# Retention with one transposition, the sample's tile at 128 rows, and scale sums in banks of their own

## The chip, the cores and the metric

The kernel runs on one core of a Trainium2 chip. The metric is device time in microseconds, from one execution's start to its end; the median of three runs stands for a kernel, and one more execution is taken by the hardware profiler. The engines are named as in the profile: PE multiplies matrices (PEld is its loading of the stationary operand), DVE and ACT work element by element and can read PE's results in PSUM, POOL works element by element in SBUF only, and SP issues most DMAs. PSUM has eight banks of 512 fp32 columns on 128 partitions.

## The reference

One layer of a streaming encoder, for 1024 frames of a new stream (the prompt) and 32 frames of a running one (the sample, behind 512 cached frames). Both go through the same weights. Cut to what matters:

```python
z = rmsnorm(x, g_norm) @ w_in                 # q, k, v of attention; q, k, v, gate of retention; 2 branch gates
o_a = diff_attn(qa, ka, va)                   # per head two softmax maps: p1 - lam * p2, times v; 8 heads
o_r = retention(qr, kr, vr)                   # per head, rotary q and k of 64, v of 128
x = x + (sigmoid(gate_a) * o_a + sigmoid(gate_r) * o_r) @ w_o
h = rmsnorm(x, g_ffn)
x = x + (silu(h @ w_ff_gate) * (h @ w_ff_up)) @ w_ff_down
x = x + sigmoid(rmsnorm(x, g_ple) @ w_ple_gate) * (p @ w_ple)

def retention_chunk(q, k, v, s0, d_mat, q_decay):
    inner = einsum('ihd,jhd->hij', q, k) * d_mat
    o = einsum('hij,jhe->ihe', inner, v)
    return o + einsum('ihd,hde->ihe', q, s0) * q_decay
```

For the prompt the state `s0` goes from chunk to chunk; for the sample it is an input. The outputs are y of both streams, the new keys and values, and the new retention states.

## The kernel before

Everything is computed to fp32's accuracy: the large products split each operand into two fp16 parts and add three fp16 matmuls (`mm3`, L471 to L473; in the first stage L713 to L715), after scaling weights by a power of two that is found from their size at run time. Transpositions and retention use fp32 on PE.

**First stage** (about the first 1,070 us): 8 heads times 9 tiles of tokens. Tiles 0 to 7 are 128 prompt tokens each; tile 8 (`i == NT - 1`) is the 32 sample tokens (`TS = 32`). For each tile there are two units. `unit_a` takes the projection's first half (attention's q, k, v, retention's q, k), norms it, splits and transposes q and k (L1045), and calls `attend`: scores (L850, L853), maximum (DVE, L860), its scaling (L862), exponential (ACT, L868, into tiles named `p`), the difference of the two maps (DVE, in place in the first map's tile), its transposition (L897) and evacuation into two fp16 parts `aT` (L904 or L906, L908), and the product with the values (L916, L917, L920). `unit_b`, four tiles behind, takes the second half (retention's v, the gates), calls `retention`, and merges both branches; the merged tile `mx` is transposed (L1208), split (L1212, L1214) and written to DRAM by SP. The number of rows of a tile is `R`, 128 or, for the sample, 32; matmuls of the sample's tile thus use 32 rows of the contraction or 32 columns of the stationary operand. For the sample `project` multiplies with weights as the stationary operand (L724), and `fold` adds the parts (L735, L737) and transposes four blocks of 32 columns back (L740).

`retention` finds a tile's rotated keys, queries and a block of zeros in `qk[..., 0:192]` as [k | q | 0]. Two transpositions (L1116), of columns 0 to 127 and 64 to 191, give [kT; qT] and [qT; 0]; one copy of both (`copy`, L388, on DVE or ACT) takes them to SBUF as `qT`. Then follow the product of k and q (L1126), the state's share (L1128), the state's increment (L1129), the mask (DVE, L1132) and the product with v (L1134). The zeros let a contraction over 128 partitions act on the 64 of q alone.

**Second stage** (from about 1,080 us): the output projection in four chunks of tokens (352, 352, 176, 176), each followed by `residual` (DVE L1524 adds to x; the sum of squares on ACT and DVE; the norm's sum over partitions on PE, L1543 and L1558; the scaling by it, DVE L1562, which reads that sum in PSUM), then the gate and up projections of 22 blocks in a scheme with 7 products for 8 (`gu_pair`, with combinations of weights on POOL, L1581, of activations, L1472, and of results, L1705 to L1720), then the first two output blocks of the down projection. `load_gu` loads and splits a block's weights: squares on ACT (L1601), their two sums added (DVE L1605), the sum over partitions on PE (`weight_scale`, L300), the power of two (L230, L234), and the split (ACT, DVE L1576). There are seven banks for products (pool `psb`, token "ps") and one, `ssb`, for the norms' sums; L300 puts its sum into column 511 of `ssb`. What an instruction waits for beyond its data follows from the tiles: accesses of one bank by different engines are kept in order.

**Third stage**: the rest of the down projection, and the last gate.

**What sets the order.** In the first two stages each piece of work is a generator that yields what it needs: an engine with an estimated time (`M`, `V`, `S`, `G` for PE, DVE, ACT, POOL), a token of a buffer ("get", "put"), an event or a delay. `Flow.run` picks the earliest by these estimates, and the instructions are issued in that order; each engine works through its own in order and waits where the data isn't there. So a changed estimate, a new token or a new instruction changes the written order of everything behind it in its stage. In `Flow`, the scale sums of the second stage hold a token "sw" of their own, and `residual` one named "ss"; that both use one bank isn't in the estimates.

Of the kernel before, what the change touches and what calls it, by code (L numbers as in the profile page):

```python
# [11 lines left out]
F32 = mybir.dt.float32  # L12
# [58 lines left out]
def M(us):  # L71
    return {"M": us}
# [111 lines left out]
def kernel(  # L184
# [104 lines left out]
    def weight_scale(amax, n, gi, tag, pool=True, norm=False, total=False, at_bank=None):  # L289
# [3 lines left out]
        if total:  # L293
            if at_bank is None:
                yield ("wait", "id")
            key, psum = at_bank or ("o", ps_o)
            yield ("get", key)
            yield M(0.06)
            ps = psum[:, 511:512] if at_bank else psum.tile([P, 512], F32, tag=key, name="mt")[:, 0:1]
            nc.tensor.matmul(out=ps, lhsT=ones16, rhs=amax, start=True, stop=True)  # L300
# [184 lines left out]
    with ExitStack() as pa:  # L485
# [35 lines left out]
        qk = hp.tile([P, NQ, 192], F32, name="qk")  # L521
        nc.gpsimd.memset(qk[:, :, P:], 0.0)
        S2 = hp.tile([P, 2, P], F32, name="S2")
        nc.gpsimd.memset(S2[64:128], 0.0)
        s02 = hp.tile([P, 2, P], F32, name="s02")
        nc.gpsimd.memset(s02[64:128], 0.0)
# [200 lines left out]
        def fold(i, ps):  # L727

            if i < NT - 1:
                return ps, "pj"  # L730
            yield ("get", "su")
            yield S(P)
            su = wk.tile([P, 2, 4, TS], F32, tag="su", name="su", bufs=1)
            psv = ps[:, 0:8 * TS].rearrange("p (g a c) -> p g a c", g=4, a=2)
            nc.scalar.copy(su[:, 1], psv[:, :, 1])  # L735
            yield V(P)
            nc.vector.tensor_tensor(out=su[:, 0], in0=psv[:, :, 0], in1=su[:, 1], op=ALU.add)  # L737
            yield M(0.5)
            for g in range(4):
                nc.tensor.transpose(out=ps[0:TS, g * P:g * P + P], in_=su[:, 0, g], identity=id32)  # L740
            yield ("put", "su")
            return ps, "pj"
# [96 lines left out]
        def attend(key, i, R, q4, sblocks, masked, vblocks, NK, sc_ap, do_ap):  # L839
# [3 lines left out]
            for ms in ((0, 1),) if NK <= 512 else ((0,), (1,)):  # L843
# [19 lines left out]
                for m in ms:  # L863
                    yield ("get", "p")
                    yield S(NK, 0.14)
                    pt = pp_.tile([P, 1024], F32, tag="p", name="p")
                    p0 = 512 * ms.index(m)
# [22 lines left out]
            for j0 in range(0, nb_, 4):  # L890
# [4 lines left out]
                for j in js:  # L895
                    n = vblocks[j][0]
                    nc.tensor.transpose(out=pt[0:n, j - j0, 0:R], in_=p0[:, j * P:j * P + n], identity=id32[0:R, 0:R])  # L897
# [86 lines left out]
        def unit_a(h, i, ps, dA, e):  # L984
            R = P if i < NT - 1 else TS
# [36 lines left out]
            nc.sync.dma_start(out=kvo[h, t0:t0 + R], in_=kv[0:R])  # L1022
# [27 lines left out]
            copy(g, kT[:, :, t0:t0 + R], ptv[:, 2:6, 0:R])  # L1050
# [58 lines left out]
        def retention(h, i, R, vr, e, box):  # L1109
            yield ("wait", ("rot", h, i))  # L1110
            yield ("get", "o")
            yield M(0.22)
            pr = ps_o.tile([P, 512], F32, tag="o", name="pr")

            for a in range(2):
                nc.tensor.transpose(out=pr[:, a * P:a * P + R], in_=qk[0:R, (h * NT + i) % NQ, 64 * a:64 * a + P], identity=id32[0:R, 0:R])  # L1116
# [9 lines left out]
            nc.tensor.matmul(out=pr[0:R, 256:256 + R], lhsT=qT[:, 0, 0:R], rhs=qT[:, 1, 0:R], start=True, stop=True)  # L1126
# [10 lines left out]
            gT = _f((1.0 - 2.0 ** (-5 - h)) ** R)  # L1137
# [15 lines left out]
        def unit_b(h, i, ps, dB, e):  # L1153
            R = P if i < NT - 1 else TS
# [52 lines left out]
            pt = ps_o.tile([P, 512], F32, tag="o", name="t")[:, 0:R]  # L1207
            nc.tensor.transpose(out=pt, in_=mx[0:R], identity=id32[0:R, 0:R])  # L1208
# [3 lines left out]
            nc.scalar.activation(mt[:, 0, 0:R], pt, AF.Copy, scale=smx)  # L1212
            yield V(P, 1.0, 0.06)
            nc.vector.scalar_tensor_tensor(out=mt[:, 1, 0:R], in0=pt, scalar=smx, in1=mt[:, 0, 0:R],  # L1214
                                           op0=ALU.mult, op1=ALU.subtract)
            nc.sync.dma_start(out=mix_d[h, :, :, t0:t0 + R], in_=mt[:, :, 0:R])
# [216 lines left out]
    with ExitStack() as pc:  # L1433
# [18 lines left out]
        with ExitStack() as pw:  # L1452
# [9 lines left out]
            ssb = pss.tile([P, 512], F32, tag="ss", name="ss")  # L1462
# [48 lines left out]
            def residual(c):  # L1511
# [29 lines left out]
                ps = ssb  # L1541
# [42 lines left out]
            def load_gu(j):  # L1584
# [22 lines left out]
                s, d = yield from weight_scale(am, 1, 1, "gu", norm=True, total=True, at_bank=("sw", ssb))  # L1607
# [24 lines left out]
            def load_dn(m):  # L1632
# [25 lines left out]
                s, d = yield from weight_scale(am, 1, None, "dn", norm=True, total=True, at_bank=("sw", ssb))  # L1658
# [161 lines left out]
            flow = Flow(dict(ps=7, ss=1, sw=1, w=3, st=2, pr=2, th=2, acc=2, sq=2))  # L1820
# [210 lines left out]
```

## Time and profile before

| what | value |
|---|---|
| median of 3 runs | 1944.28 us (1943.98 to 1944.51) |
| profiled execution | 1944.48 us |
| its span, first to last instruction | 1942.7 us |
| PE, DVE, ACT, POOL busy | 1886.0, 1511.3, 1065.4, 688.8 us |
| PE's matmuls and loads | 14267 each |
| granted TensorE clock | 0.995 |

A busy time is the time in which an engine had at least one instruction in work. Matmuls overlap, so the duration of one is longer than its share of PE. A form such as "128*32 128x512" of a matmul is rows of the contraction by columns of the stationary operand, and then the moving operand.

### The profile page before, as it was taken

The numbers are of one execution on the slowest core, as the hardware profiler recorded it, in microseconds if no ns is written. First come the engines' busy times: TensorE is split into PE (matmuls) and PEld (weight loads), VectorE is DVE, ScalarE is ACT, GpSimd is POOL, SyncE is SP. The second block draws the span as 40 slices with busy tenths as digits, with TensorE's granted clock in tenths as the row PEclk, the third lists the DMA queues.
The fourth block names the chain that finished last, engine by engine and source line by source line (L and its number), as shares of the span: only waits on it lengthen the run. The fifth ranks groups of instructions, "written<-read, shape, count | busy, mean of one in ns | idle before, by whom it ended". The sixth has DMA issues, their size and how long they took to land.

```text
span 1942.7 us, 38400 instructions
## 1 busy us (share of the span) xinstructions
PE 1886.0 (97%) x14267; PEld 1219.2 (63%) x14267; DVE 1511.3 (78%) x3947; ACT 1065.4 (55%) x2788; POOL 688.8 (35%) x1169
## 2 busy tenths in 40 slices
PE   6899999999999999999999998999999999999999
PEld 3465555655555555556566685777777776666665
DVE  7888878787787777877887579999999986753364
ACT  6766666666666666665666345555555552111132
POOL 2654435454444454444542058322323210000010
PEclk9999999999999999999999998999999999999999
DMA  6222112111121121221113721222111107211031
GB/s 205 70 64 75 62 28 63 57 49 63 33 79 57 31 82 36 55 80 29 61 57 132 267 68 34 78 89 86 69 66 45 66 31 266 73 61 64 24 131 49
DMA packets 71947, 147.43 MB, mean 76 GB/s; under 512 B 25264, under 2 KB 52016, under 8 KB 63824
## 3 DMA queue, kind: packets, MB, share of 16 engines
q1 hardware_dynamic: 71760, 144.98, 22.4%
q8 instruction: 112, 1.84, 0.4%
q14 instruction: 75, 0.61, 0.1%
HBM read 113.61 MB, written 31.34 MB: 75 GB/s over the span
## 4 chain that ended last, share of the span: by engine, by line
PE 77%; DVE 11%; POOL 5%; ACT 4%; issue 2%; DMA 1%; SPq 0%; POOLq 0%; DVEq 0%; ACTq 0%
PE ps L471 9%; PE ps L472 9%; PE ps L473 9%; PE pj L713 8%; PE pj L715 8%; PE pj L714 8%; PE ps L1448 4%; PE ps L1447 4%; PE ps L1446 4%; ACT p L868 2%; PE sc L850 1%; PE t L897 1%; PE sc L853 1%; POOL qkr L749 1%; DVE nm L860 1%
## 5 line engine op out<-in xcount | busy, mean ns | idle before, releaser
L713 PE MATMUL pj<-w,xh 128*128 128x512 f16 x1024 | 390.1, 381 | 0.0
L714 PE MATMUL pj<-w,xh 128*128 128x512 f16 x1024 | 389.5, 380 | 0.0
L715 PE MATMUL pj<-w,xh 128*128 128x512 f16 x1024 | 389.3, 380 | 0.0
L471 PE MATMUL ps<-mixs,w 128*128 128x352 f16 (+1 forms) x960 | 261.9, 278 | 1.2 <-ACT pws L1324 1.2
L472 PE MATMUL ps<-mixs,w 128*128 128x352 f16 (+1 forms) x960 | 261.9, 278 | 0.0
L473 PE MATMUL ps<-mixs,w 128*128 128x352 f16 (+1 forms) x960 | 261.8, 278 | 0.0
L471 PEld LDWEIGHTS <-w 128*128 128x128 f16 x1728 | 170.2, 98 | 63.9 <-ACT mixs L1478 6.4
L473 PEld LDWEIGHTS <-w 128*128 128x128 f16 x1728 | 170.0, 98 | 54.2 <-issue 2.7
L472 PEld LDWEIGHTS <-w 128*128 128x128 f16 x1728 | 169.9, 98 | 51.7 <-issue 2.2
L715 PEld LDWEIGHTS <-xh 128*128 128x128 f16 x1024 | 100.4, 98 | 121.9 <-issue 1.7
L1581 POOL TENSOR_TENSOR st<-st 128x512 f32<-128x512 f32 x66 | 85.8, 1301 | 251.1 <-DVE w L1576 187.0
L868 ACT ACTIVATE p<-sc,nb,scs 128x256 f32<-128x256 f32 (+7 forms) x128 | 106.1, 829 | 83.3 <-POOL nb L862 61.1
L713 PEld LDWEIGHTS <-xh 128*128 128x128 f16 x1024 | 101.2, 99 | 76.3 <-issue 2.8
L472 PE MATMUL ps<-tT,w 128*128 128x352 f16 (+1 forms) x528 | 143.7, 277 | 2.6 <-DVE tT L1472 2.6
L714 PEld LDWEIGHTS <-xh 128*128 128x128 f16 x1024 | 100.4, 98 | 71.7 <-issue 1.1
L471 PE MATMUL ps<-tT,w 128*128 128x352 f16 (+1 forms) x528 | 143.8, 277 | 0.0
L473 PE MATMUL ps<-tT,w 128*128 128x352 f16 (+1 forms) x528 | 143.6, 277 | 0.0
L1576 DVE SCALAR_TENSOR_TENSOR w<-st,gus,w 128x512 f16<-128x512 f32 x132 | 140.5, 1065 | 0.1
L860 DVE TENSOR_REDUCE nm<-sc 128x2 f32<-128x256 f32 (+6 forms) x112 | 102.7, 917 | 24.1 <-PE sc L853 22.0
L1448 PE MATMUL ps<-a,w 128*128 128x352 f16 x312 | 97.5, 313 | 0.5 <-DVE w L1667 0.5
L1446 PE MATMUL ps<-a,w 128*128 128x352 f16 x312 | 97.5, 312 | 0.0
L1447 PE MATMUL ps<-a,w 128*128 128x352 f16 x312 | 97.5, 312 | 0.0
(430 smaller groups left out, 4856.1 us busy)
## 6 DMA issues: line engine op xcount, KB each, us to landing
st<-in_win_dram SPq DMA_DIRECT2D x30, 1024.0 KB, 5.0
st<-in_wgu_dram SPq DMA_DIRECT2D x22, 1024.0 KB, 4.9
st<-in_wdn_dram SPq DMA_DIRECT2D x16, 704.0 KB, 4.6
out_dram<-kv SPq DMA_DIRECT2D x64, 128.0 KB, 1.7
a_d<-a SPq DMA_DIRECT2D x9, 528.0 KB, 2.7
b<-a_d SPq DMA_DIRECT2D x9, 528.0 KB, 8.9
mixs<-mix_d SPq DMA_DIRECT2D x8, 528.0 KB, 5.8
pw_d<-pws SPq DMA_DIRECT2D x12, 352.0 KB, 5.0
```

The source lines that it names most:

```text
L471: nc.tensor.matmul(out=ps, lhsT=wh, rhs=ah, start=first, stop=False)
L472: nc.tensor.matmul(out=ps, lhsT=wh, rhs=al, start=False, stop=False)
L473: nc.tensor.matmul(out=ps, lhsT=wl, rhs=ah, start=False, stop=last)
L713: nc.tensor.matmul(out=ps, lhsT=xhi, rhs=w[:, k, 0], start=(k == 0), stop=False)
L714: nc.tensor.matmul(out=ps, lhsT=xhi, rhs=w[:, k, 1], start=False, stop=False)
L715: nc.tensor.matmul(out=ps, lhsT=xh[:, k, 1, t0:t0 + P], rhs=w[:, k, 0], start=False, stop=(k == KD - 1))
L860: nc.vector.tensor_reduce(out=nm[0:R, mc], in_=pv, axis=AX.X, op=ALU.max, negate=True)
L868: nc.scalar.activation(pt[0:R, 0:NK], ps[0:R, p0:p0 + NK], AF.Exp, bias=nb[0:R, m:m + 1], scale=sc_ap[0:R], accum_out=Z[0:R, m:m + 1])
L1446: nc.tensor.matmul(out=ps, lhsT=wt[:, 0, j], rhs=a[:, 0, cs], start=(first and j == js[0]), stop=False)
L1447: nc.tensor.matmul(out=ps, lhsT=wt[:, 1, j], rhs=a[:, 0, cs], start=False, stop=False)
L1448: nc.tensor.matmul(out=ps, lhsT=wt[:, 2, j], rhs=a[:, 1, cs], start=False, stop=(last and j == js[-1]))
L1576: nc.vector.scalar_tensor_tensor(out=w[:, i, 1], in0=src, scalar=s, in1=w[:, i, 0], op0=ALU.mult, op1=ALU.subtract)
```

## The change

In `retention` the zeros leave `qk`, which is now [k | q]. One transposition gives [kT; qT]. Two copies take it out: the q half, partitions 64 to 127, goes to partitions 0 to 63 of one of two standing tiles `qz`, whose lower 64 partitions were set to zero at the start, and the whole goes to `qT`. The products use `qz` where they used the second transposition.

The sample's tile is handled as 128 rows: `R` is 128 everywhere in `unit_a`, `unit_b`, `attend` and `retention`, and a new `RT`, 32 for the sample, is used where results are written to memory or to a shared tile. `fold` transposes from a standing tile `suz` of four blocks of 128 columns, of which columns 32 to 127 stay zero, so the tile's rows 32 to 127 are zero from there on. The last block of keys and values of the sample has 128 rows in place of 32, and 96 columns of the first map's tile `p` are set to zero by POOL for it.

In the second stage `weight_scale` takes a fresh bank for each sum: one of the seven of the products for the first four blocks of the gate and up projections, and the norms' own for the later ones and for the down projection. The token "sw" goes; the sums now hold "ps" or "ss". `residual` takes its bank per chunk.

```diff
@@ weight_scale
-            ps = psum[:, 511:512] if at_bank else psum.tile([P, 512], F32, tag=key, name="mt")[:, 0:1]
+            ps = psum.tile([P, 512], F32, tag=key, name="mt")[:, 0:1]
@@ tiles of the first stage
-        qk = hp.tile([P, NQ, 192], F32, name="qk")
-        nc.gpsimd.memset(qk[:, :, P:], 0.0)
+        qk = hp.tile([P, NQ, P], F32, name="qk")
+        qz = [hp.tile([P, P], F32, name="qz%d" % j) for j in range(2)]
+        for j in range(2):
+            nc.gpsimd.memset(qz[j][64:128], 0.0)
...
+        suz = hp.tile([P, 4, P], F32, name="suz")
+        nc.gpsimd.memset(suz, 0.0)
@@ fold
-            su = wk.tile([P, 2, 4, TS], F32, tag="su", name="su", bufs=1)
+            su = wk.tile([P, 4, TS], F32, tag="su", name="su", bufs=1)
             psv = ps[:, 0:8 * TS].rearrange("p (g a c) -> p g a c", g=4, a=2)
-            nc.scalar.copy(su[:, 1], psv[:, :, 1])
+            nc.scalar.copy(su, psv[:, :, 1])
             yield V(P)
-            nc.vector.tensor_tensor(out=su[:, 0], in0=psv[:, :, 0], in1=su[:, 1], op=ALU.add)
+            nc.vector.tensor_tensor(out=suz[:, :, 0:TS], in0=psv[:, :, 0], in1=su, op=ALU.add)
             yield M(0.5)
             for g in range(4):
-                nc.tensor.transpose(out=ps[0:TS, g * P:g * P + P], in_=su[:, 0, g], identity=id32)
+                nc.tensor.transpose(out=ps[:, g * P:g * P + P], in_=suz[:, g], identity=id32)
@@ attend
                     pt = pp_.tile([P, 1024], F32, tag="p", name="p")
+                    if NK % P and not m:
+                        nc.gpsimd.memset(pt[:, NK:NK + P - NK % P], 0.0)
...
-                    nc.tensor.transpose(out=pt[0:n, j - j0, 0:R], in_=p0[:, j * P:j * P + n], identity=id32[0:R, 0:R])
+                    nc.tensor.transpose(out=pt[0:n, j - j0, 0:R], in_=pm[0][0:R, j * P:j * P + n], identity=id32[0:R, 0:R])
@@ unit_a (unit_b likewise, with RT in its write of mixT)
-            R = P if i < NT - 1 else TS
+            R, RT = P, P if i < NT - 1 else TS
...
-            nc.sync.dma_start(out=kvo[h, t0:t0 + R], in_=kv[0:R])
+            nc.sync.dma_start(out=kvo[h, t0:t0 + RT], in_=kv[0:RT])
...
-            copy(g, kT[:, :, t0:t0 + R], ptv[:, 2:6, 0:R])
+            copy(g, kT[:, :, t0:t0 + RT], ptv[:, 2:6, 0:RT])
...
-                vblocks.append((TS, vh[0:TS, i, 0], vh[0:TS, i, 1]))
+                vblocks.append((P, vh[:, i, 0], vh[:, i, 1]))
@@ retention
-            yield M(0.22)
+            yield M(0.11)
             pr = ps_o.tile([P, 512], F32, tag="o", name="pr")
-            for a in range(2):
-                nc.tensor.transpose(out=pr[:, a * P:a * P + R], in_=qk[0:R, (h * NT + i) % NQ, 64 * a:64 * a + P], identity=id32[0:R, 0:R])
-            qT = wk.tile([P, 2, P], F32, tag="qT", name="qT")
-            g = yield either(V(256), S(256, -0.06))
-            copy(g, qT[:, :, 0:R], pr[:, 0:2 * P].rearrange("p (a c) -> p a c", a=2)[:, :, 0:R])
+            nc.tensor.transpose(out=pr[:, 0:P], in_=qk[:, (h * NT + i) % NQ], identity=id32)
+            q0 = qz[(h * NT + i) % 2]
+            g = yield either(V(128), S(128, -0.06))
+            copy(g, q0[0:64], pr[64:128, 0:P])
+            g = yield either(V(128), S(128, -0.06))
+            qT = wk.tile([P, P], F32, tag="qT", name="qT")
+            copy(g, qT, pr[:, 0:P])
...
-            nc.tensor.matmul(out=pr[0:R, 256:256 + R], lhsT=qT[:, 0, 0:R], rhs=qT[:, 1, 0:R], start=True, stop=True)
+            nc.tensor.matmul(out=pr[:, 256:384], lhsT=qT, rhs=q0, start=True, stop=True)
             if S_in is not None:
-                nc.tensor.matmul(out=por, lhsT=qT[:, 1, 0:R], rhs=S_in, start=True, stop=False)
-            nc.tensor.matmul(out=pr[:, 384:512], lhsT=qk[0:R, (h * NT + i) % NQ, 0:P], rhs=vr[0:R], start=True, stop=True)
+                nc.tensor.matmul(out=por, lhsT=q0, rhs=S_in, start=True, stop=False)
+            nc.tensor.matmul(out=pr[:, 384:512], lhsT=qk[:, (h * NT + i) % NQ], rhs=vr, start=True, stop=True)
@@ unit_b
-            pt = ps_o.tile([P, 512], F32, tag="o", name="t")[:, 0:R]
-            nc.tensor.transpose(out=pt, in_=mx[0:R], identity=id32[0:R, 0:R])
+            pt = ps_o.tile([P, 512], F32, tag="o", name="t")
+            nc.tensor.transpose(out=pt[:, 0:P], in_=mx, identity=id32)
+            pt = pt[:, 0:RT]
@@ residual
-            ssb = pss.tile([P, 512], F32, tag="ss", name="ss")
...
-                ps = ssb
+                ps = pss.tile([P, 512], F32, tag="ss", name="ss")
@@ load_gu, load_dn
-                s, d = yield from weight_scale(am, 1, 1, "gu", norm=True, total=True, at_bank=("sw", ssb))
+                s, d = yield from weight_scale(am, 1, 1, "gu", norm=True, total=True, at_bank=("ps", psb) if j < 4 else ("ss", pss))
...
-                s, d = yield from weight_scale(am, 1, None, "dn", norm=True, total=True, at_bank=("sw", ssb))
+                s, d = yield from weight_scale(am, 1, None, "dn", norm=True, total=True, at_bank=("ss", pss))
@@ second stage
-            flow = Flow(dict(ps=7, ss=1, sw=1, w=3, st=2, pr=2, th=2, acc=2, sq=2))
+            flow = Flow(dict(ps=7, ss=1, w=3, st=2, pr=2, th=2, acc=2, sq=2))
```

More of the change, by code (lines that the diff above doesn't have):

```diff
@@ L1136, in retention @@
             yield ("set", ("ret", h, i))
-            gT = _f((1.0 - 2.0 ** (-5 - h)) ** R)
+            gT = _f((1.0 - 2.0 ** (-5 - h)) ** (P if i < NT - 1 else TS))
             yield V(128)
@@ L1153, in unit_b @@
         def unit_b(h, i, ps, dB, e):
-            R = P if i < NT - 1 else TS
+            R, RT = P, P if i < NT - 1 else TS
             t0 = i * P
@@ L1211, in unit_b @@
             mt = hp.tile([P, 2, P], F16, tag="mixT", name="mixT", bufs=4)
-            nc.scalar.activation(mt[:, 0, 0:R], pt, AF.Copy, scale=smx)
+            nc.scalar.activation(mt[:, 0, 0:RT], pt, AF.Copy, scale=smx)
             yield V(P, 1.0, 0.06)
-            nc.vector.scalar_tensor_tensor(out=mt[:, 1, 0:R], in0=pt, scalar=smx, in1=mt[:, 0, 0:R],
+            nc.vector.scalar_tensor_tensor(out=mt[:, 1, 0:RT], in0=pt, scalar=smx, in1=mt[:, 0, 0:RT],
                                            op0=ALU.mult, op1=ALU.subtract)
-            nc.sync.dma_start(out=mix_d[h, :, :, t0:t0 + R], in_=mt[:, :, 0:R])
+            nc.sync.dma_start(out=mix_d[h, :, :, t0:t0 + RT], in_=mt[:, :, 0:RT])
             yield ("later", ("mix", 2.2))
```

## The prediction

> **What bounds the kernel now.** I read the page's header first, then the busy time in stretches, the waits of PE, and PE's instructions in order of time. The stretches (columns: length, then PE, PEld, DVE, ACT, POOL busy, then granted clock, share of the DMA engines, GB/s):
>
> ```profile
> span 1942.7 us, 38400 instructions
> 75.00:1065.00 990.00, 980.06 (x7190) 573.16 (x7189) 789.64 (x2406) 649.60 (x1927) 460.12 (x923) 1.00 0.19 58
> 1153.00:1265.00 112.00, 97.44 (x862) 75.30 (x861) 108.17 (x225) 62.83 (x146) 67.07 (x69) 0.94 0.16 54
> ```
>
> From 75 to 1065 us (all but the first tiles of attention and retention) PE has 10 us without work in 990, and every other engine has at least 200: a step taken from PE there should come off the end. From 1153 to 1265 it is DVE that has no time left (108.2 of 112). The change touches the first of these stretches in two ways and the second in one. A busy PE isn't a full PE, because matmuls overlap: so I read what an instruction costs PE from its start to the next one's start.
>
> **Part 1, retention with one transposition.** In a full tile, PE in order of time:
>
> ```profile
> 394.00 0.38 PE L1116 MATMUL pr<-cst_sb,qk 128*128 128x128 f32 x2
> ...
> 395.29 0.38 PE L715 MATMUL pj<-w,xh 128*128 128x512 f16 x1
> 395.51 0.38 PE L1126 MATMUL pr<-qT 128*128 128x128 f32 x2
> ...
> 396.18 0.38 PE L713 MATMUL pj<-w,xh 128*128 128x512 f16 x1
> 464.93 0.60 PE L897 MATMUL t<-cst_sb,p 128*128 128x128 f32 x4
> 465.37 0.50 PE L1045 MATMUL t<-id,qst 128*128 128x128 f16 x6
> 465.70 0.28 PE L1116 MATMUL pr<-cst_sb,qk 128*128 128x128 f32 x1
> ```
>
> Four fp32 transpositions (L897) take 465.37 - 464.93 = 0.44 us from start to start, 0.11 each. One goes in each of 64 full tiles: **-7.0 us** (the sample's is in part 2). The copies behind it, by form (busy, mean ns):
>
> ```profile
> L388 ACT COPY qT<-pr 128x256 f32<-128x256 f32 x46 | 17.1, 372 | 20.5 <-PE pr L1116 20.1
> L735 ACT COPY su<-pj 128x128 f32<-128x128 f32 x16 | 4.4, 274 | 3.5 <-PE pj L724 3.4
> ```
>
> One copy of 372 ns becomes two of about 274: +0.17 us in 64 tiles, 11 us spread over ACT and DVE, and the first matmul (L1126) waits for the later one. What covers it is the projection's matmuls, which PE runs between the transposition and L1126: in the tile shown 1.51 us pass, of which the transpositions take 0.38 and the copy 0.37, so some 0.76 are spare. Between 0 and 0.17 us in each of 64 tiles could show (11 us at most); nearer to 0, since the written order plans the second copy in: I take +0.5. A copy from partitions 64-127 to 0-63 has no row; I give it the price of L735, which is nearest to it in size, type and source.
>
> **Part 2, the sample's tile at 128 rows.** The sample's 32 tokens are the ninth tile of each of 8 heads. Its matmuls use fewer rows or columns of the array, and the trace shows what that costs:
>
> ```profile
> 452.09 0.38 PE L715 MATMUL pj<-w,xh 128*128 128x512 f16 x1
> 452.40 0.25 PE L1126 MATMUL pr<-qT 128*32 128x32 f32 x2
> ...
> 453.21 0.39 PE L713 MATMUL pj<-w,xh 128*128 128x512 f16 x1
> ```
>
> L715 is followed after 0.31 us, where in the full tile it is 0.22: entering another shape costs 0.09, and leaving it is of the same kind. Retention's six matmuls with L715 take 1.12 us; the full tile's take 0.89, although two of its six are four times as wide. Padded: **-0.23** per head. The other groups of one sample tile:
>
> ```profile
> 415.27 0.38 PE L715 MATMUL pj<-w,xh 128*128 128x512 f16 x1
> 415.58 0.23 PE L916 MATMUL po<-vcs,aT 128*32 128x128 f16 x1
> ...
> 416.83 0.23 PE L850 MATMUL sc<-kT,q 128*128 128x128 f16 x1
> 450.45 0.38 PE L715 MATMUL pj<-w,xh 128*128 128x512 f16 x1
> 450.76 0.31 PE L1116 MATMUL pr<-cst_sb,qk 32*128 32x32 f32 x2
> 451.00 0.39 PE L713 MATMUL pj<-w,xh 128*128 128x512 f16 x1
> 408.75 0.43 PE L897 MATMUL t<-cst_sb,p 32*128 32x32 f32 x4
> 409.12 0.33 PE L1208 MATMUL t<-cst_sb,mx 128*128 128x128 f32 x1
> ```
>
> Attention times values, 15 matmuls: 416.83 - 415.27 - 0.22 = 1.34. A full step of that width and type is (465.70 - 465.37)/6 = 0.055 (L1045), so 15 cost 0.83: **-0.51**. Retention's two transpositions: 451.00 - 450.45 - 0.22 = 0.33 becomes one of 0.11: **-0.22**. Six groups remain (the scores of the two maps, p's transpositions, 4 and 1, the mix's, retention's last matmuls): each loses a way in and out, 0.19, and the six transpositions among them grow from (409.12 - 408.75 - 0.09)/4 = 0.07 to 0.11: -1.14 + 0.24, **-0.9**. The six transpositions of q and k gain 0.19 and grow by about as much: 0. The fold's (L740) stream 128 columns already: 0. Per head 0.23 + 0.51 + 0.22 + 0.9 = 1.86, in 8 heads -14.9 us. Full forms in a busy stream often take a little more than these best steps (0.2 us per head, an allowance of mine), so I take **-13.5**, with -10 and -16 as bounds.
>
> What part 2 adds to other engines:
>
> ```profile
> L904 ACT ACTIVATE aT<-t,lsc 128x512 f16<-128x512 f32 x25 | 17.3, 690 | 17.0 <-PE t L897 16.9
> L904 ACT ACTIVATE aT<-t,lsc 128x128 f16<-128x128 f32 x15 | 5.5, 367 | 1.6 <-PE t L897 1.6
> L908 DVE SCALAR_TENSOR_TENSOR aT<-t,lsc,aT 128x512 f16<-128x512 f32 x48 | 35.7, 744 | 1.2 <-ACT aT L904 0.7
> L908 DVE SCALAR_TENSOR_TENSOR aT<-t,lsc,aT 128x128 f16<-128x128 f32 x24 | 8.2, 343 | 0.1
> L522 POOL MEMSET qk<- x1: 417/417/417, 0.7 to 0.7; 128x384 f32 x1
> ```
>
> The evacuations of the transposed p widen from 128 to 512 elements, +0.32 and +0.40 us per head, and the smaller ones (its last block, q, retention's copies, the masked product) by about as much together: 1.5, in 8 heads 12 us over ACT and DVE. The 200 us that DVE has free hide it; without that cover it is up to 12. The zeroing behind p's first map is 96 columns on POOL, under 0.42 us, 8 times; behind it in POOL's queue wait the maxima's scaling and the norms' roots, and for those ACT. The memsets at the start take the place of one of 0.42 and lie before 5 us, where nothing has been loaded. For all this +0.5.
>
> One rule of the Trainium skill speaks against padding: "TensorE: Matmul & The Clock Gate", section "LDWEIGHTS (loading the stationary operand)", has a load's time go by its columns, P/1.2 ns: 27 ns for 32 of them, 107 for 128. By it, an estimate, 37 widened loads in each of 8 heads add up to 24 us where nothing hides them, and the sum would be near 1946. What the loads do here (mean ns of one):
>
> ```profile
> L916 PEld LDWEIGHTS <-aT 128*128 128x128 f16 x288 | 28.2, 98 | 5.3
> L916 PEld LDWEIGHTS <-aT 128*32 128x32 f16 x32 | 2.9, 96 | 2.6 <-DVE S L1146 1.3 <-issue 0.9 <-DVE mixT L1214 0.4
> ```
>
> Both widths take the same, 98 and 96 ns, with matmuls 0.055 apart: loads overlap, and the steps above hold them already.
>
> **Part 3, the scale sums in other banks.** In the stretch from 1153 us PE stands (waits: total, times, longest; then PE and DVE in order of time):
>
> ```profile
> PE ss L300 <- DVE xf L1562: 8.4, 2, 6.3
> 1179.62 0.16 PE L300 MATMUL ss<-wamh,cst_sb 128*128 128x1 bf16 x1 [6.31 <-DVE xf L1562]
> 1180.19 0.50 PE L473 MATMUL ps<-mixs,w 128*128 128x352 f16 x1
> 1180.48 0.50 PE L471 MATMUL ps<-mixs,w 128*128 128x352 f16 x1
> 1176.18 0.14 DVE L1605 TENSOR_TENSOR wamh<-gam 128x1 bf16<-128x1 f32 x1
> ```
>
> L300 puts a weight's sum into a corner of the bank that the norm's scaling (L1562) still reads; that costs 6.3 and 2.1 us. Behind the first, matmuls of 352 columns start 0.29 us apart, where L1045's rate (0.055 for 128) gives 0.15; the stretch's granted clock of 0.94 is 0.06 x 112 = 6.7 us of clock lost, part of it while PE stood, so some 4 us of slow matmuls. With a bank of its own L300 still needs L1605, done at 1176.3, and then DVE is next in line: it is busy 108.2 of 112 us and every product needs DVE's sums and split weights, so PE can win little more than what DVE idles, 3.8. I take **-2.5**. Bounds: -12.4 (both stalls and the slow matmuls gone) and +4 (the sum now takes one of the seven banks of the products, which DVE frees late once: another 2.1 and as much of slow matmuls).
>
> **Sum** against the profiled execution's 1944.5 us (span 1942.7 and 1.8 around it; the runs' median, 1944.28, is 0.2 lower): -7.0 + 0.5 - 13.5 + 0.5 - 2.5 = -22, **1922 us**.
>
> **Rivals.**
> (a) DVE isn't the next bound, and all of part 3's stalls go: 9.9 more, 1912. For it: DVE's work there is put into another order too. Against: it is 97% busy.
> (b) The shorter PE meets ACT and DVE: half of their 23 us of new work comes onto the path, 1934. For it: p goes from DVE to PE to ACT to DVE to PE. Against: 200 us free on DVE.
> (c) The padding doesn't do what it says: the 0.09 us belongs to the type or the moment, not to the shape, and stays. Then only the widening is left, some 0.5 us per head, and -7 + 4 + 1 - 2.5 gives 1940. Against: L916 is f16 between f16 and pays it.
> (d) Slower: in every second of 72 tiles both of retention's copies queue behind one instruction of 744 ns (L908), and PE, in order, waits at L1126 with the projections behind it: 0.17 + 1.49 - 0.76 = 0.9 us, 32 in all, 1954. It decides from 0.31 us per tile. Against: 20.1 of the 20.5 us that ACT idled before this copy was for its transposition, so it rarely queues.
> (e) The widened loads don't overlap: 98 - 55 = 43 ns for each of 37 in 8 heads, 13 us, 1935; the skill's rule above is this one. Against: the full forms' steps of 0.055.
>
> **Chances.** Forecast 0.67, (a) 0.10, (b) 0.11, (c) 0.05, (d) 0.05, (e) 0.02. The forecast's own bounds (part 1 to +4, part 2 from -16 to -10, part 3 from -12.4 to +4) don't all fall on one side; 1911 to 1936 holds them for the most part and (a), (b) and (e). A measurement of this kernel tells 0.2% (3.9 us) from no change: faster 0.92, same 0.03, slower 0.05.
>
> **What would show it.** L1116 with 72 instructions, and no 32*128, 128*32 or 32*32 form left before 1065 us; that stretch some 20 us shorter with PE as full as now; L300 waiting for L1562 nowhere, and DVE still over 95% busy for the 100 us behind. Wrong: a first stretch that shrinks by 7 or less (c), PE waiting at L1126 for a copy (d), steps over 0.055 in the sample's L916 (e), or more than 10 us gained after 1065 (a).

## The result, and the profile after

| | before | after |
|---|---|---|
| median of 4 runs, same chip | 1944.39 us (1943.98 to 1944.96) | 1926.31 us (1925.08 to 1927.92) |
| ratio, 95% interval | | 0.9907 [0.989, 0.9924] |
| profiled execution, span | 1944.5, 1942.7 us | 1926.3, 1924.5 us |
| first matmul of projection group 20 (of 128) | 191.2 us | 191.3 us |
| last matmul of the projections | 1052.0 us | 1032.3 us |
| first matmul of the output projection | 1082.7 us | 1064.5 us |
| second scale sum (L300) of the gate and up weights | 1179.6 us | 1159.7 us |
| seventh scale sum | 1283.4 us | 1265.2 us |

The change gains 18.1 us; 22 were forecast. The lower rows are starts of single matmuls in the profiled executions, in the order of time. All of the gain is made in the first stage (19.7 us at its end); the way into the second stage gives 1.4 back. At the second scale sum the kernels are 19.9 us apart, but from the seventh on 18.2 again. The line numbers have moved: L1116 is L1122, L1126 L1135, L916 and L917 L923 and L924, L920 L927, L1208 L1217, L1562 L1571, L1605 L1614.

The stretches of the kernel after (length, then PE, PEld, DVE, ACT, POOL busy, clock, share of the DMA engines, GB/s), beside the page's header:

```profile
span 1924.5 us, 38354 instructions
75.00:1040.00 965.00, 954.48 (x7080) 570.81 (x7079) 792.07 (x2426) 660.44 (x1966) 448.82 (x913) 1.00 0.19 57
1135.00:1250.00 115.00, 99.80 (x921) 78.76 (x919) 112.02 (x238) 64.61 (x151) 67.83 (x69) 0.97 0.18 61
```

PE is as full as before: 10.5 of 965 us without an instruction, where it was 10 of 990. DVE is still the fullest engine of the second stretch, 112.0 of 115. The transposition of retention by its line (instructions, then ns min/median/max, first and last start, form), and the sample's product with the values in PE's order of time:

```profile
L1122 PE MATMUL pr<-cst_sb,qk x72: 272/273/308, 81.4 to 1040.4; 128*128 128x128 f32 x72
```

```profile
407.11 0.22 PE L923 MATMUL po<-vcs,aT 128*128 128x128 f16 x1
407.17 0.22 PE L924 MATMUL po<-vcs,aT 128*128 128x128 f16 x1
...
407.67 0.39 PE L927 MATMUL po<-vcs,aT 128*128 128x128 f16 x4
407.89 0.22 PE L927 MATMUL po<-vh,aT 128*128 128x128 f16 x1
407.95 0.38 PE L718 MATMUL pj<-w,xh 128*128 128x512 f16 x1
```

There are 72 transpositions where there were 144, all of one shape. The 15 products with the values take 407.95 - 407.11 = 0.84 us; before they took 1.34, and 0.83 was forecast. Then the waits of PE from 1040 to 1250 us (total, times, longest), and two of them in order of time:

```profile
PE mt L300 <- DVE wamh L1614: 7.0, 4, 3.1
PE ps L472 <- DVE tT L1481: 2.9, 1, 2.9
PE ps L472 <- POOL mixs L1481: 2.4, 1, 2.4
PE mt L275 <- DVE wam L432: 1.8, 1, 1.8
PE ss L1552 <- DVE gus L315: 1.7, 1, 1.7
```

```profile
1159.73 0.16 PE L300 MATMUL mt<-wamh,cst_sb 128*128 128x1 bf16 x1 [3.07 <-DVE wamh L1614]
1166.85 0.46 PE L1552 MATMUL ss<-cst_sb,acc 128*44 128x1 f32 x8 [1.68 <-DVE gus L315]
```

L300 waits for the norm's scaling (L1571) nowhere. It waits for its own operand instead, the sum L1614, 7.0 us where the old wait was 8.4, and PE stands for other products of DVE and POOL beside it.

To see what PE's time is made of, I added up the steps from each PE instruction's start to the next one's, from projection group 20 to the last matmul of the projections. A step is split into what its kind takes in a full stream (0.216 us for 512 columns, 0.056 for 128 in f16, 0.110 for 128 in fp32), and an excess: put down to a **gap** when PE stood idle, to **shape** when the array's shape in use changed with it, and to **rest** otherwise. It is worked out from some 6,100 steps of each trace. The totals and gaps are read off; how the remainder divides into stream, shape and rest hangs by 2 to 3 us on the price put on narrow forms (with the median step of each narrow form the first row has 819.7, 18.4 and 9.9).

| kernel | total us | full stream | shape | gaps | rest |
|---|---|---|---|---|---|
| before | 860.7 | 822.6 | 16.7 | 12.8 | 8.7 |
| after | 841.1 | 818.3 | 2.0 | 13.6 | 7.1 |

Shape gives 14.7 and the stream 4.3 (one transposition less, but wider matmuls for the sample). That is near the forecast, and so it looked as if all terms were right. The parts taken alone said otherwise.

### The profile page after: what moved, and what is told of

The parts are those of the page before. It is cut to its first block, busy times and chain, and to the rows that moved or that the text cites. A ratio compares the mean times of both kernels' runs of the same rounds, so it can differ in the third digit from the quotient of the medians.

```text
span 1924.5 us, 38354 instructions
## 1 busy us (share of the span) xinstructions
PE 1865.0 (97%) x14195; PEld 1220.5 (63%) x14195; DVE 1518.9 (79%) x3987; ACT 1080.7 (56%) x2836; POOL 680.9 (35%) x1163
## 4 chain that ended last, share of the span: by engine, by line
PE 72%; DVE 14%; POOL 6%; ACT 4%; issue 2%; DMA 1%; SPq 0%; POOLq 0%; DVEq 0%; ACTq 0%
PE ps L471 9%; PE ps L472 9%; PE ps L473 9%; PE pj L718 7%; PE pj L719 7%; PE pj L720 7%; PE ps L1458 4%; PE ps L1457 4%; PE ps L1456 4%; DVE nm L865 2%; ACT p L875 1%; PE sc L855 1%; DVE w L464 1%; PE sc L858 1%; POOL qkr L754 1%
```

## The experiments

The kernels were timed in four groups, each on one chip and in turn with the kernel before, whose median was 1943.8 to 1944.6 us in each group. My theory at the outset: the three parts are worth what the sum says, each by itself. The rival: a gain belongs to something that the parts have in common, so they don't add up.

**The parts one by one.** Part 1 alone leaves the sample at 32 rows:

```diff
+            nc.tensor.transpose(out=pr[:, 0:R], in_=qk[0:R, (h * NT + i) % NQ], identity=id32[0:R, 0:R])
+            copy(g, q0[0:64, 0:R], pr[64:128, 0:R])
+            copy(g, qT[:, 0:R], pr[:, 0:R])
```

> The kernel before with retention's one transposition and two copies alone; the sample's tile keeps its 32 rows and the scale sums their bank. My theory (PE sets the end of the first stage, the copies are covered): 64 steps of 0.11 us on PE less, and one of the sample's two in 8 tiles, against some 0.5 us that shows of the second copy: 6 to 8 us faster than before. Rival (the copies' 11 us on ACT and DVE come onto the path, as in the prediction's rival d): no gain, or slower, with waits of PE for L388's copies that add up to 7 us or more.

Measured: 1942.24 us, ratio 0.9991 [0.9982, 0.9999]: far less than the 6 to 8 us of the theory. Nor does PE wait 7 us or more for the copies, as its rival asks: it waits 0.2 us at L1131 for `qT` from 191 to 1050 us. Part 2 alone keeps `qk` at 192 columns and both transpositions, with R = 128:

> The kernel before with the sample's tile at 128 rows alone; retention keeps two transpositions and one copy. My theory (entering and leaving another shape of the array costs PE 0.09 us, and the widened work hides): 11 to 14 us faster than before, the first stage shorter by as much. Rival c (the 0.09 us belongs to the type and stays): 2 to 6 us slower, as only the widening is left. Rival b (the wider evacuations come onto PE's path): 3 to 8 us faster.

Measured: 1945.41 us, ratio 1.0007 [0.9998, 1.0017], 1.6 us slower; rival (c)'s 2 to 6 is nearest. Parts 1 and 2 without part 3:

> The changed kernel with the scale sums back in the norms' bank. If part 3 is worth nothing, this takes what the changed kernel takes, 1926 us within 1.5. If part 3 gains its 2.5 us, 1928.5; if part 3 costs (a bank of the products' seven), 1924 or less. If the parts of the first stage add up, its gain is that of part 1 alone and part 2 alone together, within 1.5 us.

Measured: 1927.73 us, ratio 0.9914 [0.9901, 0.9928]. Part 3 alone, only the second stage's banks:

> The kernel before with the scale sums in other banks alone; the first stage is untouched. My theory (DVE is the next bound there): between 3 us faster and no change; L300 no longer waits for the norm's scaling L1562, and other waits of PE for DVE take its place. Rival a (the stalls and the slow matmuls behind them were all that bank's): 8 to 12 us faster. After the changed kernel's trace, where the second stage takes as long as before, I lean to no change at all.

Measured: 1943.12 us, ratio 0.9994 [0.9985, 1.0002]. Part 3 is worth about 1.2 us, or 1.4 behind the others (1927.73 to 1926.31), too little to tell from nothing. The profiled executions agree on its size and show where it stays: at the second scale sum the kernel after is 3.6 us ahead of the one without part 3 (1159.73 against 1163.35), at the seventh 1.0 (1265.24 against 1266.28). But -1.5 for part 1 and +1.6 for part 2 (1945.41 against 1943.78 in that group) don't make the -16.1 of both. Here my theory fell. In the table of steps part 2 alone has the forecast's shape term (1.9 left), but 17.9 us of gaps, 4.3 more than the kernels with both parts; and it loses time on the way into the second stage, which takes 37.4 us from the last projection to the first matmul of the output projection where before takes 30.8 (PE, order of time, two matmuls of 352 columns behind the wait):

```profile
1076.87 0.37 PE L275 MATMUL mt<-cst_sb,wam 128*1 128x128 f32 x1 [4.93 <-DVE wam L432]
1077.03 0.50 PE L471 MATMUL pj<-w 128*128 128x352 f16 x1
1077.33 0.50 PE L472 MATMUL pj<-w 128*128 128x352 f16 x1
```

Neither part touches this place. What both touch is the written order: the planner's estimates differ, so each of these kernels is a different list of instructions on every engine. That can be tested, because the planner's numbers can be set without changing an instruction.

**Four kernels in one order.** The estimates are set so that every kernel gets the order of the one with parts 1 and 2. Part 1 with the sample at 32 rows, in that order, is the part 1 kernel with

```diff
-                g = yield either(S(nj * R, 0.05), V(nj * R, 1.0, 0.06))
+                g = yield either(S(nj * P, 0.05), V(nj * P, 1.0, 0.06))
...
-                yield V(nj * R, 1.0, 0.06)
+                yield V(nj * P, 1.0, 0.06)
```

> Part 1 of the change with the sample tokens' tile at 32 rows as before, but with the planner's estimates for the 32-row operations set to those of 128 rows, so that every engine's instructions come out in the order of the kernel with parts 1 and 2 (1927.73 us). The only difference to that kernel is then the shape of the sample's work. If a change of array shape on TensorE costs what the prediction says, this kernel takes 13 to 15 us more than it: 1941 to 1943 us, with the shape-switch time back in the first stage. If part 2 is worth nothing, as part 2 alone (1945.41 us) seemed to say, and the 16 us of both parts come from a lucky order, it stays within 3 us of 1927.7.

Measured: 1935.43 us, ratio 0.9956 [0.9943, 0.9968]: 7.7 more than both parts, between the two expectations. Part 2 with two transpositions, in that order:

```diff
-            yield M(0.22)
+            yield M(0.11)
...
-            g = yield either(V(256), S(256, -0.06))
+            g = yield either(V(128), S(128, -0.06))
+            yield either(V(128), S(128, -0.06))
```

> Part 2 of the change with two transpositions and the wide copy of before, but with the planner told of one transposition and two narrow copies, so that the order comes out nearly as in the kernel with parts 1 and 2 (1927.73 us); what differs is one more fp32 transposition in each of 72 tiles and one copy less. If a transposition is worth 0.1 us of a full TensorE, it takes 6 to 8 us more: 1934 to 1936 us, and some 10 us less than part 2 alone, 1945.41 us, which has the same instructions in another order. If part 2 itself takes the time back, whatever the order, it stays at 1943 to 1946 us.

Measured: 1930.59 us, ratio 0.9926 [0.9913, 0.994]: 2.9 more than both parts, less than either expectation. The kernel before with both edits, so that only its order changes:

> The kernel before with three of the planner's numbers set as the changed kernel has them (one transposition, two narrow copies, 128-row tiles); not one instruction is changed, only the order in which they are written, which is now that of the kernel with parts 1 and 2 (1927.73 us). With the part 1 and the part 2 kernel in the same order (1930.59 and 1935.43 us) this closes the square. If the two parts add up in one order, it takes 1927.7 + 2.9 + 7.7 = 1938.3 us, some 6 us less than before, which is then what the order brought. If they don't add up and the order brought nothing, it takes 1944 us.

Measured: 1942.22 us, ratio 0.9986 [0.9977, 0.9995], between the two expectations. (In that text the two times stand in reverse: the kernel with part 1 is the one of 1935.43, that with part 2 the one of 1930.59; the sum is the same.) The traces bear the name of the section out: from the first projections to the output projection PE runs the same operations in the same order in both kernels of a column. The square, in medians of runs:

| in one order | two transpositions | one transposition |
|---|---|---|
| sample at 32 rows | 1942.22 | 1935.43 |
| sample at 128 rows | 1930.59 | 1927.73 |

| in one order, steps of PE | total us | full stream | shape | gaps | rest |
|---|---|---|---|---|---|
| neither part | 853.8 | 821.7 | 16.5 | 9.1 | 6.5 |
| part 1 | 849.6 | 815.1 | 16.7 | 10.4 | 7.4 |
| part 2 | 843.4 | 825.1 | 1.7 | 10.3 | 6.2 |
| both | 841.1 | 818.3 | 2.0 | 13.6 | 7.1 |

Three things follow. First, taken alone each part is worth nearly what was forecast: part 1 -6.8 us, part 2 -11.6. The forecast, with the sample's transposition counted in part 1 as it is here, is -7.4 and -12.1.

Second, they overlap: on top of each other the medians make them worth -2.9 and -7.7. How much they overlap is uncertain, since each of the four times carries an interval of some 2 us to either side. The steps of the single traces say less: 4.2 and 10.4 us off the stage alone, 2.3 and 8.5 on top. Stream and shape change by nearly the same amount for a part, whether the other is there or not; what differs is the gaps, which grow from 9.1 to 13.6. With less work PE waits more, for the element work of other engines. The longest waits of PE from 191 to 1050 us with neither part, then with both:

```profile
PE t L1209 <- POOL mx L1204: 1.2, 3, 0.6
PE t L1209 <- DVE aT L908: 1.0, 2, 0.5
```

```profile
PE t L1217 <- POOL mx L1212: 1.9, 5, 0.6
PE po L923 <- DVE aT L915: 1.4, 3, 0.5
PE t L1217 <- DVE aT L915: 1.3, 2, 0.7
```

Third, the instructions of part 1 alone take 1942.24 us in one order and 1935.43 in the other, and those of part 2 alone 1945.41 and 1930.59: the order of the single parts had eaten 7 and 15 us.

**Only the order.** If this is so, the changed kernel must lose time by an order alone. One estimate is put back, no instruction is changed:

```diff
-            yield M(0.11)
+            yield M(0.22)
             pr = ps_o.tile([P, 512], F32, tag="o", name="pr")
```

> The changed kernel with one number of the planner put back, the 0.22 us it reserves on TensorE for the transposition of retention; no instruction is changed, only the order in which they are written. If the written order alone is worth several us, as the sums of the two parts alone say, this kernel differs from the changed one by 3 to 15 us, most likely upward (1929 to 1941 us). If order is worth nothing, it stays within 1 us of 1926.3.

Measured: 1939.32 us, ratio 0.9975 [0.9966, 0.9984]: 13.0 us lost. Its first stage by stretch, and the two largest waits of PE from 191 to 1050 us:

```profile
75.00:1055.00 980.00, 963.65 (x7086) 570.03 (x7085) 790.66 (x2352) 685.85 (x2024) 464.64 (x939) 1.00 0.18 57
```

```profile
PE t L1217 <- DVE mx L1212: 2.7, 6, 0.4
PE mt L300 <- DVE wamh L430: 2.1, 5, 0.4
```

PE stands for 16.4 us where the changed kernel's stands for 10.5, and by steps its gaps are 24.6 us against 13.6, its rest 11.4 against 7.1. No wait is long; there are 44 in place of 21, each at most 0.4 us, and on many different instructions.

**The price of a shape.** The last block of values of the sample goes back to 32 rows, in the same order:

```diff
-                vblocks.append((P, vh[:, i, 0], vh[:, i, 1]))
+                vblocks.append((TS, vh[0:TS, i, 0], vh[0:TS, i, 1]))
```

> The changed kernel with the last block of values of the sample's attention at 32 rows again: same order, same count, three or so multiplications and one transposition of a head back on 32 rows, which is one stretch of another array shape in each of 8 heads. At the 0.3 to 0.5 us for a head that the prediction's row of attention times values gives, it takes 2.4 to 4 us more: 1928.7 to 1930.3 us. If the price hangs on something other than the rows in use, nothing changes: 1925.5 to 1927.

Measured: 1928.66 us, ratio 0.992 [0.9906, 0.9933], 2.35 more than the changed kernel. PE in order of time, the same products as above:

```profile
408.50 0.22 PE L923 MATMUL po<-vcs,aT 128*128 128x128 f16 x1
408.55 0.22 PE L924 MATMUL po<-vcs,aT 128*128 128x128 f16 x1
408.70 0.22 PE L923 MATMUL po<-vh,aT 32*128 32x128 f16 x1
408.77 0.21 PE L924 MATMUL po<-vh,aT 32*128 32x128 f16 x1
408.92 0.40 PE L927 MATMUL po<-vcs,aT 128*128 128x128 f16 x4
409.25 0.23 PE L927 MATMUL po<-vh,aT 32*128 32x128 f16 x1
409.40 0.39 PE L718 MATMUL pj<-w,xh 128*128 128x512 f16 x1
```

The step into 32 rows is 0.15 where it is 0.05 within a shape (408.50 to 408.55, 408.55 to 408.70), the step out of it 0.15 again. Same type, same place in the order, only the rows differ: the 0.09 us belongs to the shape, and rival (c) is out. The shape term of the steps goes from 2.0 to 4.4 us, the time by as much. The Trainium skill, "TensorEngine Tiling (Array Packing)", section "Key Properties", says that changing the tiling mode drains TensorE; it names no price, and this trace agrees with a drain of some 0.09 us each way.

Not every narrow form pays it. The fold's fp32 transpositions use 32 columns over all 128 rows, and in the kernel before they come and go at the full pace, 0.22 behind L715 and 4 x 0.11 until the next:

```profile
193.59 0.38 PE L715 MATMUL pj<-w,xh 128*128 128x512 f16 x1
193.81 0.60 PE L740 MATMUL pj<-cst_sb,su 128*32 128x128 f32 x4
194.25 0.38 PE L713 MATMUL pj<-w,xh 128*128 128x512 f16 x1
```

The products on 32 columns (L916, L850, L1126 of the sample) do pay. So what costs is not any change of the form in the profile's rows; why these transpositions are free, no run here shows.

**One more transposition.** The changed kernel with a second transposition whose result nobody reads, unknown to the planner:

```diff
             nc.tensor.transpose(out=pr[:, 0:P], in_=qk[:, (h * NT + i) % NQ], identity=id32)
+            nc.tensor.transpose(out=pr[:, 128:256], in_=qk[:, (h * NT + i) % NQ], identity=id32)
```

> The changed kernel with one transposition more in each of 72 tiles, into columns that nobody reads, unknown to the planner: same order, both copies as they are. If the first stage runs at TensorE's pace, 72 x 0.11 = 7.9 us more: 1933 to 1935 us; then the 2.9 us that part 1 gave at this order say that the second copy took some 4 us back. If TensorE's gaps give way when its work grows, 2 to 5 us more, 1928 to 1931 us, and the second copy costs about nothing.

Measured: 1931.45 us, ratio 0.9929 [0.9917, 0.9942]: 5.1 us more than the changed kernel, between the two expectations. By steps the stream grows by 6.8 us and the gaps shrink by 2.8: two thirds of the expected 7.9 us are paid in time, and part of the rest fills gaps. The kernel in one order with part 2 only (1930.59) has the same PE work, but one wide copy and no part 3: so the second copy costs 0.9 us plus the 1.4 of part 3, some 2.3, about as uncertain as it is large.

**DVE as the bound of the second stage.** The sum L1614 that L300 waits for goes from DVE to ACT, which has made its two inputs:

```diff
-                yield V(1)
+                yield S(1)
                 am = sm(1, "wamh", 3, BF16)
-                nc.vector.tensor_tensor(out=am, in0=am2[:, 0:1], in1=am2[:, 1:2], op=ALU.add)
+                nc.scalar.activation(am, am2[:, 0:1], AF.Identity, bias=am2[:, 1:2], scale=1.0)
```

> The changed kernel with the two-column sum of a gate weight's squares taken from VectorE to ScalarE, which has just made them: the wait of the scale's matmul for it (7.0 us in four places between 1135 and 1250 us) should go. If VectorE bounds that stretch, as the prediction says, the wait moves to another product of VectorE and 0 to 2 us are gained: 1924.3 to 1926.5 us. If the wait itself was what cost the time, 5 to 7 us: 1919 to 1921 us. The order of the second stage changes a little with it, which may be worth 2 us either way.

Measured: 1921.68 us, ratio 0.9881 [0.9867, 0.9894], 4.6 less than the changed kernel: more than the 0 to 2 that DVE's bound allows, less than the wait's 7.0. Its waits of PE from 1040 to 1250 us and its stretch:

```profile
PE ss L1552 <- DVE acc L1544: 4.4, 1, 4.4
PE ps L471 <- ACT w L1582: 2.8, 1, 2.8
PE ps L473 <- DVE w L1585: 2.4, 1, 2.4
```

```profile
1135.00:1250.00 115.00, 104.95 (x971) 82.37 (x970) 110.29 (x240) 68.10 (x161) 70.26 (x72) 0.94 0.18 61
```

The wait did move to other products of DVE and ACT, but they cost less: in the same 115 us PE runs 971 matmuls where it ran 921, with DVE nearly as busy as before (110.3 against 112.0). PE's busy time, 105.0 against 99.8, overstates this, as the granted clock is lower, 0.94 against 0.97. The first stage is unchanged (last projection matmul 0.1 us apart); at the first scale sum the kernels still run 0.3 us apart, at the seventh 4.5, and that stays to the end. The order of the second stage changes with this edit as well: the second scale sum is now written behind L1552 and comes 5.9 us later than in the changed kernel (1165.6 against 1159.7). So how much belongs to the sum's place and how much to the new order stays open.

**Truer estimates.** The kernel just shown, with the planner's numbers for retention taken from the trace. The copies of the changed kernel, by tile and form (instructions, ns min/median/max, first and last start):

```profile
L388 ACT COPY qT<-pr x42: 266/266/271, 196.7 to 985.5; 128x128 f32<-128x128 f32 x42
L388 DVE COPY qT<-pr x19: 269/284/292, 282.8 to 1023.1; 128x128 f32<-128x128 f32 x19
```

```diff
-            g = yield either(V(128), S(128, -0.06))
+            g = yield either(V(128, 1.0, 0.08), S(128, 0.06))
             copy(g, q0[0:64], pr[64:128, 0:P])
-            g = yield either(V(128), S(128, -0.06))
+            g = yield either(V(128, 1.0, 0.08), S(128, 0.06))
...
-            yield M(0.66)
+            yield M(0.33)
...
-            yield M(0.22)
+            yield M(0.11)
             nc.tensor.matmul(out=por, lhsT=inn[0:R, 0:R], rhs=vr[0:R], start=(S_in is None), stop=True)
```

> The kernel with the gate sum on ScalarE (1921.68 us), with the planner's numbers for retention set to what the trace shows: 0.27 to 0.28 us for each of the two copies on ScalarE or VectorE (it reckons with 0.15 and 0.20), and 0.11 us on TensorE for each fp32 matmul (it reckons with 0.22). No instruction is changed, only the order. If truer numbers make a better order, the first stage gets 3 to 8 us shorter, 1914 to 1919 us. If the order is a matter of chance, as the 13 us of one changed number suggest, the stage may as well come out up to 15 us longer: 1922 to 1937 us.

Measured: 1910.47 us (1908.82 to 1910.9), ratio 0.9824 [0.9811, 0.9838]. It is 11.2 us under the kernel with the sum on ACT and 15.8 under the changed kernel: the fastest of all, and faster than either expectation. Its first stage:

```profile
75.00:1040.00 965.00, 958.91 (x7141) 578.75 (x7140) 801.22 (x2433) 668.86 (x1985) 450.70 (x921) 1.00 0.20 61
```

PE stands for 6.1 of 965 us where it stood for 10.5; by steps the gaps are 8.4 us against 13.6. Against the kernel with the sum on ACT, the last projection matmul comes 8.2 us earlier and the first of the output projection 10.6. One run can't say that truer numbers make better orders in general, only that this one is 11 us better.

## Why the prediction was right, and where it wasn't

The time, 1926.31, lies 4.3 us above the forecast and inside the range. In the forecast's own terms, from the kernels in one order:

| term | forecast | measured |
|---|---|---|
| parts 1 and 2, retention and padding, in one order | -19.5 | -14.5 |
| the new order of the first stage | none | -2.2 |
| part 3 | -2.5 | -1.4 |
| sum | -22 | -18.1 |

**What PE gained.** The two kernels with two transpositions, with the sample at 32 and at 128 rows (1942.22 and 1930.59 us), run the same operations in the same order on PE, so each group of the sample's matmuls can be set beside itself, from the start of the matmul before it to the start of the one behind it. The medians of the 8 heads:

| group of the sample's matmuls, us per head | forecast | by steps |
|---|---|---|
| attention times values | -0.51 | -0.50 |
| scores of the two maps | -0.38 | -0.37 |
| retention's six | -0.23 | -0.24 |
| retention's transposition, way in and out | -0.11 | -0.11 |
| retention's last | -0.19 | -0.18 |
| the mix's transposition | -0.15 | -0.16 |
| p's transpositions, 4 and 1 | -0.18 | -0.14 |
| q, k and the fold | 0 | 0.00 |

Over the whole first stage these groups take 12.6 us less (a little under 8 medians, as some heads gain less). The sample's second transposition, which the forecast counts in part 2 and the square in part 1, is another 8 x 0.11 = 0.9. So part 2 took 13.5 us off PE's steps, what the forecast had after its allowance. (The table of steps has less, 11.4: its window leaves out the first head's sample tile.) Part 1 takes 64 x 0.11 = 7.0 off the full tiles, as forecast. So PE's steps shrank by the forecast 20.5 us.

**Part 1.** Its +0.5 for the second copy was too little (some 2.3, by the uncertain estimate above). PE waits at L1135 for a copy of `qT` once from 191 to 1050 us, for 0.7 us: rival (d) asked for that in every second tile.

**Part 2.** The price of entering and leaving a shape, 0.09 each, was read from three steps and holds over the stage. The widened loads don't show: the products with the values still start 0.056 apart (407.11 to 407.67 for ten), which puts rival (e) out. The rule that the prediction takes from the Trainium skill, "TensorE: Matmul & The Clock Gate", section "LDWEIGHTS (loading the stationary operand)", would have cost 24 us, an estimate, if nothing hid the loads; no such cost shows in this trace.

**The step that failed** is "a step taken from PE there should come off the end", with "the 200 us that DVE has free hide it". Both read a whole stage, and they are why the two terms for what might show of the new element work, +0.5 for each part, were too small. Of the 20.5 us that PE's steps lost in one order, 14.5 reached the end: 6.0 did not, where 1.0 had been set. In the table of steps stream and shape lose 821.7 + 16.5 - 818.3 - 2.0 = 17.9 us, but the total only 12.7, as gaps and rest grow by 5.1. From group 20 to the last projection PE's waits of more than 0.15 us go from 15 (4.8 us) to 21 (7.7 us), for `mx` on POOL and DVE, for the evacuation `aT`, for ACT's `th` and `p` and for one copy: short chains within a tile, which the free time of an engine over the stage says nothing about. This is a smaller piece of rival (b), which put half of the 23 us of new element work onto the path.

**What had no term at all** is the order. The prediction said that the written order plans the second copy in, and otherwise took the order as given. The runs show 13 us from one changed number, 7 and 15 for the two parts alone, 11 for truer estimates. Before to after it was worth some 2 us in favour (by the interval of the kernel before in the new order, 1.0 to 4.5), so the forecast came out near. That this term came out small was luck: with one of the planner's numbers left as it was, the changed kernel took 1939.32 us, outside the range.

**Part 3.** L300's wait for the norm's scaling went, and DVE's products took its place, as said; -1.4 against -2.5, and rival (a) didn't come. The reason given for the ceiling, that PE can win little more than the 3.8 us that DVE idles, doesn't hold: with the sum on ACT and DVE still busy for 110.3 of 115 us the end comes 4.6 us earlier, 6.0 together with part 3. I read this as follows, though no run shows it by itself: much of what DVE does there can be done later, and what counts is which of its instructions come first.

## What to carry to other kernels

Where a planner writes the order, a change has two effects, and they can be of one size: time the old instructions in the new order (only the planner's numbers changed) before a gain or a loss is given to an edit, and don't expect parts that were timed alone to add up. Work taken from an engine that is 99% busy comes off the end only until its neighbours' chains are met; here 20.5 us of PE's steps gave 14.5, and an edit that took 4.2 us off the stage by itself took 2.3 on top of another. And an engine that is 97% busy isn't by that alone the bound: another place for one small sum, and the order that came with it, still gave 4.6 us.

## What the runs showed of the hardware

Going from matmuls on 128 rows and columns to ones on 32 rows costs PE about 0.09 us, and so does the way back; products on 32 columns pay the same (L715 to L916 in the kernel before, 0.31 for 0.22). That is as much as one and a half f16 matmuls of 128 columns. So a few small matmuls on 32 rows can be slower than full ones. The fold's transpositions on 32 columns pay nothing.

Behind 4.93 us without work PE's matmuls of 352 columns start 0.29 us apart, twice the 0.15 of a full stream. The granted clock there, in the kernel with part 2 alone, is 0.50 from 1077 to 1085 us. In the kernel after it is the same behind 3.07 us without work (0.29 apart from 1160.2 to 1163.1, the clock 0.67 from 1160 to 1165), but behind 1.68 us they start 0.15 apart at once: a long wait is dearer than it is long.

And half as many partitions made a copy no shorter:

```profile
L388 ACT COPY qz<-pr x51: 262/263/263, 209.9 to 1012.0; 64x128 f32<-64x128 f32 x51
L388 DVE COPY qz<-pr x10: 292/293/294, 196.4 to 1022.5; 64x128 f32<-64x128 f32 x10
```

263 ns on ACT and 293 on DVE for 64 partitions, where 128 took 266 and 284. The narrow copy also moves its rows from partitions 64 to 127 down to 0 to 63; no run here separates the two. Splitting a copy by partitions, as this change does, adds the full price of a second one.
